# A two-layer model in one kernel: when the expert gather begins, where attention's modulation rows run, and a third raw weight buffer

## The chip, the cores and the metric

The kernel runs on one core of a Trainium2 chip. The metric is the device time of one execution in microseconds (us). Before the change it is 3226.53 us, the median of three runs (3223.47 to 3227.59).

## The reference

Two layers on 512 tokens of width 1024, float32, batch 1. Each layer has a mixer and a PEER feed-forward part, and each of these four parts has a norm whose shift, scale and gate are worked out from a conditioning vector `c` (its 3072 outputs are 24 rows of 128, "modulation rows", in what follows).

```python
def ada_modulation(c, w, b):
    mod = jax.nn.silu(c) @ w + b
    shift, scale, gate = jnp.split(mod, 3, axis=-1)
...
for layer in range(DEPTH):
    shift, scale, gate = ada_modulation(c, mw, mb)      # of the mixer's norm
    h = rms_norm(x, g) * (1.0 + scale) + shift
    x = x + gate * mixer(h, ...)    # layer 0: rglru_mixer, layer 1: fox_mixer
    shift, scale, gate = ada_modulation(c, mw, mb)      # of the feed-forward's norm
    h = rms_norm(x, g) * (1.0 + scale) + shift
    x = x + gate * peer_ffn(h, ...)
```

`rglru_mixer` is a gated linear recurrence behind a short convolution. `fox_mixer` is causal softmax attention with 16 heads of 64 and a forget gate. The feed-forward part picks 16 of 16384 experts for each token and each of 8 heads:

```python
        cand = (v1[..., :, None] + v2[..., None, :]).reshape(TOKEN_CHUNK, PEER_HEADS, PEER_TOPK * PEER_TOPK)
        top_s, top_c = lax.top_k(cand, PEER_TOPK)
        expert = e1 * PEER_KEYS + e2
        g = jax.nn.softmax(top_s, axis=-1)
        u = jnp.take(expert_u, expert, axis=0)
        act = jax.nn.gelu(jnp.einsum('thkd,td->thk', u, xc), approximate=False)
        return jnp.einsum('thk,thkd->td', g * act, jnp.take(expert_v, expert, axis=0))
```

## The kernel before

**Matmuls and weights.** Every product is made of three: weights and activations are split into a high and a low part, and high×high, high×low and low×high are added up (L275 to L277 in the projections, L847 in the experts' second product). All weights come through one object, `Stream` (L123): SyncE (SP) loads a block into a raw buffer `wraw`, ScalarE (ACT) writes its high part `whi`, VectorE (DVE), or GpSimd (POOL) in the queries, the low part `wlo` (L209, L210). There are two raw buffers and, only in the expert loop, a third (`stream.third`); splits run three blocks ahead of their use.

**Stages** (start times from the trace): a norm, the recurrence `lru` (28 us) and its output projection `out_proj` (210); a norm and `peer` of layer 0 (297); a norm and `fox` of layer 1 (1586) with `out_proj` (1906); a norm and `peer` of layer 1 (1960 to the end). Inside `peer` follow one another: `queries` (projection, scores `sps` against the subkeys, top-k on DVE), the first products of 56 of the 128 chunks of 128 experts ("first ups", stored in DRAM for the loop) beside the routing and the dense gates, and the loop over 128 chunks.

**The loop.** For three of the four tiles of 128 tokens all experts are computed, chunk by chunk, six chunks ahead with the first product (`expert_in`). `gated` (L834) multiplies a chunk's activations `at` with its gates, which come back from DRAM in tiles `gtile` of 8 chunks, 1.5 MB, loaded by SP (L818); then ACT and DVE make `wh` (L838) and `wl` (L840). The fourth token tile gathers its experts' rows instead (`gathered`): 128 indirect DMAs of 512 KB for u and 128 for v, issued by POOL (L766) into a ring of eight buffers with the tag "gat", and a pinned DVE instruction for each (L772, L782).

**Background work.** Generators give up work piece by piece: `bg.pump(credit)` draws pieces until their costs (1.2 for a row) have used up the credit. The gather is drawn in the loop, with 3.75 for a chunk that needs its first product and 1.15 for a stored one (`PUMP`). Modulation rows are made by `mod_gen` (L159): a 512 KB load `mw` and a DVE dot product (L174) for each row, with a small operation that puts the result in a column (L178 to L181). Layer 1's mixer norm (`l1_mix`) gets its first 16 rows in layer 0's queries (loaded by SP) and its 8 gate rows in `fox` (loaded by POOL, one buffer), followed there by 18 rows of `l1_ffn`. `row_of` (L187) sends the gate through DRAM: SP writes `line`, POOL loads it back, spread over the partitions, as `grow` (L193).

**Order.** A scheduler reorders instructions on each engine, except for those marked with `keep_in_program_order`, which keep their order among themselves: the dot products, the gather's DVE instructions, the norm's `rs` on POOL (L230) and the first two `gated`.

Of the kernel before, what the change touches and what calls it, by code (L numbers as in the profile page):

```python
# [4 lines left out]
F32 = mybir.dt.float32  # L5
# [29 lines left out]
NEARLY = 16  # L35
PUMP = (3.75, 1.15)
AHEAD = 6
# [85 lines left out]
class Stream:  # L123
# [11 lines left out]
    def fill(self, last):  # L135

        g, nc = self.g, self.g.nc
        last = min(last, len(self.blocks) - 1)
        while len(self.parts) <= last:
            (src, shape, n), b = self.blocks[len(self.parts)]  # L140
            if b == 0:
                self.loads += 1
                src_pool = self.third if self.third and self.loads % 3 == 0 else g.wraw
                self.raw = src_pool.tile([128, n, *shape], F32, name="wraw", tag="wraw")
                nc.sync.dma_start(self.raw, src)
            raw = self.raw[:, b]
            hi = g.wsp.tile([128, *shape], F32R, name="whi", tag="whi")
            lo = g.wsp.tile([128, *shape], F32R, name="wlo", tag="wlo")
            split(g, hi, lo, raw, nc.gpsimd if self.on_pool else nc.vector)
            self.parts.append((hi, lo))  # L150
# [7 lines left out]

def mod_gen(g, pool, mwT, sub, rows, bufs=2, pin=True, queue=None):  # L159

# [4 lines left out]
    def load(r):  # L165
        wf = pool.tile([128, D], F32, name="mw", tag="gat", bufs=bufs)
        (queue or nc.sync).dma_start(wf, mwT[r])
        return wf
# [132 lines left out]

def out_proj(g, psum, y, nk, grow, bg):

    T = g.nc.tensor
    yhi, ylo = y
    load_x(g)
    for half in range(2):
        acc = [psum.tile([128, 512], F32, name=f"oacc{half}{t}") for t in range(TC)]
        pairs = [(k, min(2, nk - k)) for k in range(0, nk, 2)]
# [61 lines left out]
def lru(g, h, conv, bias, lam, during, grow_fn, after):  # L371
# [3 lines left out]
    with pool(tc, name="lruy", bufs=1) as ly:  # L375
        yhi = ly.tile([128, NR, S], F32R, name="yhi")
        ylo = ly.tile([128, NR, S], F32R, name="ylo")
        with pool(tc, name="lru", bufs=1) as lp, pool(tc, name="lruw", bufs=2) as lw:
# [27 lines left out]
            with pool(tc, name="lps", bufs=4, space=PSUM) as psum, \  # L406
                    pool(tc, name="lps2", bufs=2, space=PSUM) as psum2:
                bg = Background(*during(lw))
                ge = {}
# [35 lines left out]
                head = proj_early(g, psum, h, 2)  # L445
                for j in range(NR):
                    ps = head.pop(0) if head else proj_t(g, psum, h)
                    xp = lw.tile([128, S + 3], F32, name="xp", tag="xp")
# [11 lines left out]
                    ps = head.pop(0) if head else proj_t(g, psum, h)  # L460
                    ge[j] = lw.tile([128, S], F32, name="ge", tag="ge", bufs=4)
                    A.activation(ge[j], ps, AF.Gelu)
# [6 lines left out]
        with pool(tc, name="mw", bufs=2) as mw, pool(tc, name="ops", bufs=1, space=PSUM) as psum:  # L469
            out_proj(g, psum, (yhi, ylo), NR, grow, Background(*after(mw)))  # L470


def finish_mixer(g, y, nk, grow, after):

    with pool(g.tc, name="ysp", bufs=1) as yp, pool(g.tc, name="mw", bufs=2) as mw, \
            pool(g.tc, name="ops", bufs=1, space=PSUM) as psum:
        yhi = yp.tile([128, nk, S], F32R, name="yhi")
        ylo = yp.tile([128, nk, S], F32R, name="ylo")
        for k in range(nk):
            split(g, yhi[:, k, :], ylo[:, k, :], y[:, k, :])  # L480
        out_proj(g, psum, (yhi, ylo), nk, grow, Background(*after(mw)))

# [53 lines left out]

def peer(g, h, u, v, grow_fn, during, nd):

# [7 lines left out]
    with pool(tc, name="pk", bufs=1) as pk:  # L546
# [32 lines left out]
        def queries(pw, pa, psum):  # L579

            early, todo = [], []
            bg = Background(*during(pw))

            def scores(hd, w, qh, ql, skh, skl):
# [10 lines left out]
            for hd in range(PH):  # L595
                if hd == 0:
                    early = proj_early(g, psum, h, 2)
                for w in range(2):
                    ps = early.pop(0) if early else proj_t(g, psum, h)
                    if w:  # L600
                        sk = g.stream.take()
                        scores(*todo.pop(), *sk)
                    qh = pw.tile([128, S], F32R, name="qh", tag="qh", bufs=3)
                    ql = pw.tile([128, S], F32R, name="ql", tag="ql", bufs=3)
                    split(g, qh, ql, ps)
                    todo.append((hd, w, qh, ql))
                    if w == 0 and hd > 0:
                        search(hd - 1)
                for c in ups_after(hd):
                    first_up(pa, psum, c)  # L610
                    if todo:
                        scores(*todo.pop(), *sk)
                    bg.pump(1.2)
            bg.finish()
            g.stream.on_pool = False
# [142 lines left out]
        def gathered(t, out):  # L758
# [5 lines left out]
            def fetch(src, j):  # L764
                rows = env["gat"].tile([128, D], F32, name="rows", tag="gat")
                nc.gpsimd.indirect_dma_start(out=rows, out_offset=None, in_=src,  # L766
                                             in_offset=bass.IndirectOffsetOnAxis(ap=ei[:, j:j + 1], axis=0))
                return rows
            for j in range(128):
                r = fetch(u, j)  # L770
# [3 lines left out]
            A.activation(act, act, AF.Gelu)  # L774
            V.tensor_mul(act, act, gt)
            for j in range(128):
                r = fetch(v, j)
# [12 lines left out]
        for t in range(nd, TC):  # L790
            rest.append([])
            late.append(gathered(t, rest[-1]))
        with pool(tc, name="pa", bufs=2) as pa, pool(tc, name="ups", bufs=3, space=PSUM) as psum:
            with pool(tc, name="qw", bufs=2) as qw:
                queries(qw, pa, psum)
            natural(g, psum, h, TC - 1, hn)
            grow = grow_fn()
            with pool(tc, name="pu", bufs=1) as pu, pool(tc, name="pw", bufs=2) as pw:
                todo = []
                bg = Background(*[route(t) for t in range(TC)], *[dense_gates(t, pu, pw, psum, todo) for t in range(nd)])  # L800
                for c in FIRST[NEARLY:]:
                    first_up(pa, psum, c)
                    bg.pump(GP)
                bg.finish()
        rguard.__exit__(None, None, None)
        with pool(tc, name="vw", bufs=2) as vw, pool(tc, name="vps", bufs=2, space=PSUM) as psum:
# [3 lines left out]
            pad(g, vw, 384)  # L810
            g.stream.third = vw
            bg = Background(*late)
# [17 lines left out]
            def gated(c):  # L830
# [7 lines left out]
                pin(A.activation(wh, at, AF.Copy))  # L838
                ready[c] = (wh, wl)
                return lambda: V.tensor_sub(wl, at, wh)  # L840

# [8 lines left out]
            def pump(i):  # L850
                bg.pump(PUMP[1] if stored(i // 2) else PUMP[0])

# [264 lines left out]
def model(tc, *aps):  # L1117
# [4 lines left out]
    with ExitStack() as ctx:  # L1122
# [17 lines left out]

        def mod(p, pool, rows=(*first, *gate), bufs=2, queue=tc.nc.gpsimd):
            return mod_gen(g, pool, a[p + "_mw"], mods[p], rows, bufs, bufs < 8, queue)

# [17 lines left out]
        with pool(tc, name="mw0", bufs=8) as mw:  # L1161
# [3 lines left out]
            lambda p: (mod("l0_mix", p, gate, MB), mod("l0_ffn", p, first[:M0], MB)), grow("l0_mix"), lambda p: (mod("l0_ffn", p, (*first[M0:], *gate)),))  # L1165
        peer(g, normed("l0_ffn"), flat("l0_u"), flat("l0_v"), grow("l0_ffn"), lambda p: (mod("l1_mix", p, first, 2, tc.nc.sync),), 3)
        fox(g, normed("l1_mix"), *arg("fox_", "fb", "qg", "kg"), lambda p: (mod("l1_mix", p, gate, 1), mod("l1_ffn", p, (*first, *gate)[:M2], 1)),
            grow("l1_mix"), lambda p: (mod("l1_ffn", p, (*first, *gate)[M2:]),))
        peer(g, normed("l1_ffn"), flat("l1_u"), flat("l1_v"), grow("l1_ffn"), lambda p: (), 3)
        drop_x(g)  # L1170
# [95 lines left out]
```

## Time and profile before

| what | value |
|---|---|
| median of the runs, us | 3226.53 |
| the profiled execution's own time, us | 3225.38 |
| its span, us | 3223.6 |
| layer 0: queries, first ups and gates, loop (starts, us) | 297, 497, 725 |
| layer 1: queries, first ups and gates, loop (starts, us) | 1960, 2147, 2373 |
| data moved by DMA | 818.97 MB, 254 GB/s on average |
| the gathers' issues of u and of v rows (POOL busy), us | 365.2 and 367.0 |

Times count from the start of the span. A row of the windows view has, behind the stretch and its length, the busy time of PE (TensorE), PEld (its weight loads), DVE, ACT and POOL in it with the count of instructions, then the clock that TensorE was granted (1.00 is full), the mean busy share of the 16 DMA engines (a little over 1 where packets overlap) and the GB/s that they moved. A row of the waits view names who waited for whom, for how long in total, how often, and the longest wait. A row of the timeline has start, length, engine and instruction, and in brackets the idle time ahead of it. `PE vacc L847 <- DVE wl L840` means that the matmul of line 847 into `vacc` waited for the VectorE instruction of line 840 that writes `wl`.

### The profile page before, as it was taken

The numbers are of one execution on the slowest core, as the hardware profiler recorded it, in microseconds if no ns is written. First come the engines' busy times: TensorE is split into PE (matmuls) and PEld (weight loads), VectorE is DVE, ScalarE is ACT, GpSimd is POOL, SyncE is SP. The second block draws the span as 40 slices with busy tenths as digits, with TensorE's granted clock in tenths as the row PEclk, the third lists the DMA queues.
The fourth block names the chain that finished last, engine by engine and source line by source line (L and its number), as shares of the span: only waits on it lengthen the run. The fifth ranks groups of instructions, "written<-read, shape, count | busy, mean of one in ns | idle before, by whom it ended". The sixth has DMA issues, their size and how long they took to land.

```text
span 3223.6 us, 44230 instructions
## 1 busy us (share of the span) xinstructions
PE 3082.9 (96%) x16192; PEld 2702.7 (84%) x16192; DVE 2578.9 (80%) x5230; ACT 1465.8 (45%) x2057; POOL 986.2 (31%) x825
## 2 busy tenths in 40 slices
PE   6998989998999999999999989999989999999999
PEld 5777889988888888888776768899978888888887
DVE  7776899997787888887568976789869788888884
ACT  5773226783333333333357743246853333333332
POOL 1002430005454544441011104430026454444430
PEclk9999999999999999999999989999999999999999
DMA  6454444679999999996332343235799999999983
GB/s 264 136 178 170 165 146 153 240 279 396 365 341 353 348 342 346 347 342 238 116 116 80 113 158 125 100 138 202 270 339 383 366 349 342 348 333 360 334 307 135
DMA packets 304778, 818.97 MB, mean 254 GB/s; under 512 B 27824, under 2 KB 156848, under 8 KB 276016
## 3 DMA queue, kind: packets, MB, share of 16 engines
q1 hardware_dynamic: 175408, 398.22, 35.0%
q0 software_dynamic: 84800, 304.65, 25.1%
q10 hardware_dynamic: 44352, 113.27, 9.3%
q8 instruction: 127, 2.08, 0.2%
q14 instruction: 91, 0.75, 0.1%
HBM read 735.03 MB, written 81.02 MB: 253 GB/s over the span
## 4 chain that ended last, share of the span: by engine, by line
PE 43%; DMA 2%; DVE 2%; issue 2%; ACT 2%; POOL 0%; DVEq 0%; ACTq 0%; POOLq 0%; SPq 0%
PE vacc L847 16%; PE pacc L277 7%; PE pacc L275 7%; PE pacc L276 7%; PE gps L727 1%; DMA gtile<-gscr 1%; DMA gscr<-st 0%; PE oacc L315 0%; PE vacc L953 0%; PE oacc L317 0%; PE oacc L316 0%; PE vacc L955 0%; PE vacc L954 0%; PE tp L1086 0%; ACT st L729 0%
## 5 line engine op out<-in xcount | busy, mean ns | idle before, releaser
L209 ACT ACTIVATE whi<-wraw 128x1024 fp32r<-128x1024 f32 (+2 forms) x646 | 666.1, 1034 | 764.5 <-PE pacc L276 349.8
L275 PE MATMUL pacc<-hhi,whi 128*128 128x384 f32 (+1 forms) x2632 | 931.5, 354 | 17.3 <-ACT at L828 9.0
L277 PE MATMUL pacc<-hhi,wlo 128*128 128x384 f32 (+1 forms) x2632 | 926.5, 352 | 5.2 <-DVE wlo L210 5.1
L276 PE MATMUL pacc<-hlo,whi 128*128 128x384 f32 (+1 forms) x2632 | 924.7, 351 | 0.0
L210 DVE TENSOR_TENSOR wlo<-wraw,whi 128x1024 fp32r<-128x1024 f32 (+1 forms) x566 | 683.2, 1210 | 229.0 <-ACT whi L209 215.7
L847 PE MATMUL vacc<-whi,wh 128*128 128x512 f32 x1536 | 603.5, 393 | 6.6 <-ACT wh L838 6.6
L847 PE MATMUL vacc<-wlo,wh 128*128 128x512 f32 x1536 | 606.3, 395 | 0.0
L847 PE MATMUL vacc<-whi,wl 128*128 128x512 f32 x1536 | 597.3, 389 | 1.5 <-DVE wl L840 1.5
L275 PEld LDWEIGHTS pacc<-hhi,whi 128*128 128x128 f32 x2632 | 500.9, 190 | 46.2 <-ACT at L828 9.3
L277 PEld LDWEIGHTS pacc<-hhi,wlo 128*128 128x128 f32 x2632 | 499.8, 190 | 31.5 <-DVE wlo L210 6.9
L276 PEld LDWEIGHTS pacc<-hlo,whi 128*128 128x128 f32 x2632 | 500.9, 190 | 29.3 <-issue 2.8
L766 POOL DMA_INDIRECT rows<-in_l_v_dram,ei x256 | 367.0, 1434 | 408.2 <-DVE accg L782 361.5
L766 POOL DMA_INDIRECT rows<-in_l_u_dram,ei x256 | 365.2, 1427 | 365.3 <-DVE rows L772 298.1
L838 ACT ACTIVATE wh<-at 128x384 fp32r<-128x384 f32 x256 | 133.9, 525 | 699.4 <-PE vacc L847 346.0
L847 PEld LDWEIGHTS vacc<-whi,wh 128*128 128x128 f32 x1536 | 288.9, 188 | 68.6 <-ACT wh L838 6.9
L847 PEld LDWEIGHTS vacc<-whi,wl 128*128 128x128 f32 x1536 | 289.0, 188 | 67.0 <-DVE wl L840 2.4
L847 PEld LDWEIGHTS vacc<-wlo,wh 128*128 128x128 f32 x1536 | 289.5, 188 | 52.6
L782 DVE SCALAR_TENSOR_TENSOR accg<-rows,act,accg 128x1024 f32<-128x1024 f32 x254 | 324.6, 1278 | 0.5
L772 DVE SCALAR_TENSOR_TENSOR rows<-rows,hn 128x1024 f32<-128x1024 f32 x256 | 304.6, 1217 | 0.0
L834 DVE TENSOR_TENSOR at<-at,gtile 128x384 f32<-128x384 f32 x256 | 140.6, 552 | 144.0 <-DMA at<-ascr 120.9
L210 POOL TENSOR_TENSOR wlo<-wraw,whi 128x1024 fp32r<-128x1024 f32 (+1 forms) x80 | 169.9, 2134 | 212.4 <-ACT whi L209 202.8
L729 ACT ACTIVATE st<-gps 128x512 f32<-128x512 f32 x192 | 185.1, 1109 | 42.0 <-PE gps L727 38.1
(268 smaller groups left out, 3397.2 us busy)
## 6 DMA issues: line engine op xcount, KB each, us to landing
wraw<-in_l_uT_dram SPq DMA_DIRECT2D x128, 1024.0 KB
wraw<-in_l_v_dram SPq DMA_DIRECT2D x128, 1024.0 KB
gscr<-st ACTq DMA_DIRECT2D x48, 1024.0 KB
gtile<-gscr SPq DMA_DIRECT2D x32, 1536.0 KB
mw<-in_l_ffn_mw_dram POOLq DMA_DIRECT2D x48, 512.0 KB
ascr<-at ACTq DMA_DIRECT2D x112, 192.0 KB
at<-ascr ACTq DMA_DIRECT2D x112, 192.0 KB
mw<-in_l_mix_mw_dram SPq DMA_DIRECT2D x32, 512.0 KB
```

Of the source, the lines that this page charges most:

```text
L209: g.nc.scalar.activation(hi, raw, AF.Copy)
L210: (eng or g.nc.vector).tensor_sub(lo, raw, hi)
L275: nc.tensor.matmul(ps, whi[:, k, :], hhi[:, k, :n], start=(k == 0), stop=False)
L276: nc.tensor.matmul(ps, whi[:, k, :], hlo[:, k, :n], start=False, stop=False)
L277: nc.tensor.matmul(ps, wlo[:, k, :], hhi[:, k, :n], start=False, stop=(k == KD - 1))
L729: A.activation(st[:, :, q * 4:q * 4 + 4].rearrange("p e t -> p t e"), gps, AF.Copy, scale=1.0 / GSCALE)
L766: nc.gpsimd.indirect_dma_start(out=rows, out_offset=None, in_=src, in_offset=bass.IndirectOffsetOnAxis(ap=ei[:, j:j + 1], axis=0))
L772: V.scalar_tensor_tensor(r, r, 1.0, hn, op0=OP.mult, op1=OP.mult, accum_out=act[:, j:j + 1]))
L782: tc.keep_in_program_order(V.scalar_tensor_tensor(acc, r, w, acc, op0=OP.mult, op1=OP.add))
L834: pin(V.tensor_tensor(at.rearrange("p (b t) -> p b t", t=16), at.rearrange("p (b t) -> p b t", t=16), gts[c // 8][:, :, c % 8, :], op=OP.m ...
L838: pin(A.activation(wh, at, AF.Copy))
L847: T.matmul(acc[t][d], x[:, ts], y[:, d, :], start=(i == 0 and x is wh and y is vh), stop=(i == PK - 1 and x is wl))
```

## The change

Four things are changed.

1. The gather of a layer waits for the loop's first gated chunk: a POOL copy into `act` reads that chunk's `at`, and it and the first eight u fetches are kept in program order.
2. All 24 rows of `l1_mix` move into layer 0's gather, between its u and its v rows; they use the gather's ring and POOL's queue, four loads ahead. Layer 0's credits are raised to 4.05 and 1.25 (`PUMPS`).
3. Every third load gets a third raw buffer in more stages: the recurrence (with three instead of four `ge` buffers), the first half of the output projections, and the queries and first ups (off for the last six).
4. In the queries the split of `ps` into `qh` and `ql` is written ahead of the scores of the half before.

```diff
-PUMP = (3.75, 1.15)
+PUMPS = ((4.05, 1.25), (3.75, 1.15))
...
-                src_pool = self.third if self.third and self.loads % 3 == 0 else g.wraw
-                self.raw = src_pool.tile([128, n, *shape], F32, name="wraw", tag="wraw")
+                raw, bufs = g.wraw, 2
+                if self.third and self.loads % 3 == 0:
+                    raw, bufs = self.third
+                self.raw = raw.tile([128, n, *shape], F32, name="wraw", tag="wraw", bufs=bufs)
...
-def mod_gen(g, pool, mwT, sub, rows, bufs=2, pin=True, queue=None):
+def mod_gen(g, pool, mwT, sub, rows, bufs=2, pin=True, queue=None, ring=None):
...
-        wf = pool.tile([128, D], F32, name="mw", tag="gat", bufs=bufs)
+        wf = pool.tile([128, D], F32, name="mw", tag="gat", bufs=ring or bufs)
...
+        g.stream.third = None if half else (third, 1)
...
+                g.stream.third = (lw, 1)
...
-                    ge[j] = lw.tile([128, S], F32, name="ge", tag="ge", bufs=4)
+                    ge[j] = lw.tile([128, S], F32, name="ge", tag="ge", bufs=3)
...
+                    qh = pw.tile([128, S], F32R, name="qh", tag="qh", bufs=3)
+                    ql = pw.tile([128, S], F32R, name="ql", tag="ql", bufs=3)
+                    split(g, qh, ql, ps)
                     if w:
                         sk = g.stream.take()
                         scores(*todo.pop(), *sk)
-                    qh = pw.tile([128, S], F32R, name="qh", tag="qh", bufs=3)
-                    ql = pw.tile([128, S], F32R, name="ql", tag="ql", bufs=3)
-                    split(g, qh, ql, ps)
...
-                    bg.pump(1.2)
-            bg.finish()
...
-                nc.gpsimd.indirect_dma_start(out=rows, out_offset=None, in_=src,
-                                             in_offset=bass.IndirectOffsetOnAxis(ap=ei[:, j:j + 1], axis=0))
+                i = nc.gpsimd.indirect_dma_start(out=rows, out_offset=None, in_=src,
+                                                 in_offset=bass.IndirectOffsetOnAxis(ap=ei[:, j:j + 1], axis=0))
+                if src is u and j < 8:
+                    tc.keep_in_program_order(i)
                 return rows
+            tc.keep_in_program_order(nc.gpsimd.tensor_copy(act[:, 127:128], env["first"][:, 0:1]))
...
+            if between:
+                yield from between(env["gat"])
...
+            g.stream.third = (pa, 1)
...
+                    if c == FIRST[-6]:
+                        g.stream.third = None
...
-            g.stream.third = vw
+            g.stream.third = (vw, 2)
...
+                env.setdefault("first", at)
...
-                bg.pump(PUMP[1] if stored(i // 2) else PUMP[0])
+                bg.pump(cost[1] if stored(i // 2) else cost[0])
...
-        peer(g, normed("l0_ffn"), flat("l0_u"), flat("l0_v"), grow("l0_ffn"), lambda p: (mod("l1_mix", p, first, 2, tc.nc.sync),), 3)
-        fox(g, normed("l1_mix"), *arg("fox_", "fb", "qg", "kg"), lambda p: (mod("l1_mix", p, gate, 1), mod("l1_ffn", p, (*first, *gate)[:M2], 1)),
+        peer(g, normed("l0_ffn"), flat("l0_u"), flat("l0_v"), grow("l0_ffn"), lambda p: mod("l1_mix", p, bufs=4, ring=8), 3, PUMPS[0])
+        fox(g, normed("l1_mix"), *arg("fox_", "fb", "qg", "kg"), lambda p: (mod("l1_ffn", p, (*first, *gate)[:M2], 1),),
             grow("l1_mix"), lambda p: (mod("l1_ffn", p, (*first, *gate)[M2:]),))
-        peer(g, normed("l1_ffn"), flat("l1_u"), flat("l1_v"), grow("l1_ffn"), lambda p: (), 3)
+        peer(g, normed("l1_ffn"), flat("l1_u"), flat("l1_v"), grow("l1_ffn"), None, 3, PUMPS[1])
```

DVE in layer 0's queries, one of the places where modulation rows (`mw`, `mdot`, `col_l_mix`) stand within the search for the best candidates (`cand`), before:

```order
L561 MAX_INDEX idxs_2427<-vals_2425,tk 128x8
L174 SCALAR_TENSOR_TENSOR mw,mdot<-mw,sc 128x1024
L572 TENSOR_TENSOR cand<-vals_2425,vals_2424 128x4x16
L181 TENSOR_TENSOR col_l_mix_147<-mdot,bias_l_mix 128x1
L174 SCALAR_TENSOR_TENSOR mw,mdot<-mw,sc 128x1024
L572 TENSOR_TENSOR cand<-vals_2425,vals_2424 128x4x2 x2
L178 TENSOR_SCALAR mdot<-mdot,bias_l_mix 128x1
L572 TENSOR_TENSOR cand<-vals_2425,vals_2424 128x4x2
L574 TENSOR_TENSOR cand<-vals_2424,vals_2425 128x4x8
```

The same place in the changed kernel:

```order
L567 MAX_INDEX idxs_2427<-vals_2425,tk 128x8
L578 TENSOR_TENSOR cand<-vals_2425,vals_2424 128x4x16
L578 TENSOR_TENSOR cand<-vals_2425,vals_2424 128x4x2 x3
L580 TENSOR_TENSOR cand<-vals_2424,vals_2425 128x4x8
L563 MAX top<-cand 128x8 x2
```

The dot products and their column operations are gone from between the candidates; the rest stands as it was. The order of `qh` and `ql` (L210, now L212) among these instructions hasn't moved.

DVE at the start of layer 0's loop, before (`at_7477` is chunk 0's tile, `rows` a gathered row, `act` its results):

```order
L210 TENSOR_TENSOR wlo<-wraw,whi 128x1024 x4
L834 TENSOR_TENSOR at_7541<-at_7541,gtile 128x384
L772 SCALAR_TENSOR_TENSOR rows,act<-rows,hn 128x1024 x2
L210 TENSOR_TENSOR wlo<-wraw,whi 128x1024
L772 SCALAR_TENSOR_TENSOR rows,act<-rows,hn 128x1024
L210 TENSOR_TENSOR wlo<-wraw,whi 128x1024
L834 TENSOR_TENSOR at_7477<-at_7477,gtile 128x384
```

And in the changed kernel, where `at_7389` is chunk 0's tile:

```order
L212 TENSOR_TENSOR wlo<-wraw,whi 128x1024 x4
L844 TENSOR_TENSOR at_7453<-at_7453,gtile 128x384
L212 TENSOR_TENSOR wlo<-wraw,whi 128x1024 x2
L844 TENSOR_TENSOR at_7389<-at_7389,gtile 128x384
L844 TENSOR_TENSOR at_7486<-at_7486,gtile 128x384
L212 TENSOR_TENSOR wlo<-wraw,whi 128x1024
L851 TENSOR_TENSOR wl<-at_7389,wh 128x384
L844 TENSOR_TENSOR at_7420<-at_7420,gtile 128x384
L777 SCALAR_TENSOR_TENSOR rows,act<-rows,hn 128x1024 x2
```

The first gathered rows now stand behind four gated chunks instead of one.

POOL in the second half of `fox`, before, where `qx` and `kx` are loads that the attention's heads need:

```order
L167 DMA mw<-in_l_mix_mw_dram 128x1024 x2
L167 DMA mw<-in_l_ffn_mw_dram 128x1024
L1046 DMA qx<-cx 4x512 x2
L193 DMA grow<-line 128x1024
L1057 DMA kx<-cx 4x512 x2
```

POOL in layer 0's loop and at the norm behind it, in the changed kernel:

```order
L773 COPY act<-at_7389 128x1
L768 DMA rows<-in_l_u_dram,ei 128x1024 x128
L169 DMA mw<-in_l_mix_mw_dram 128x1024 x24
L768 DMA rows<-in_l_v_dram,ei 128x1024 x128
L195 DMA grow<-line 128x1024
L232 TENSOR_TENSOR rs<-ms,mhalf 128x1 x4
```

The copy stands ahead of all gathers, the 24 `mw` loads between u and v, and `grow` has moved out of `fox` to just ahead of the norm's four `rs`.

More of the change, by code (lines that the diff above doesn't have):

```diff
@@ L299, in out_plan, with out_proj @@
     return plan
-def out_proj(g, psum, y, nk, grow, bg):
+def out_proj(g, psum, y, nk, grow, bg, third):
     T = g.nc.tensor
@@ L446, in lru @@
                 for j in range(NR):
+                    if j == NR - 1:
+                        g.stream.third = None
                     ps = head.pop(0) if head else proj_t(g, psum, h)
@@ L469, in lru @@
         with pool(tc, name="mw", bufs=2) as mw, pool(tc, name="ops", bufs=1, space=PSUM) as psum:
-            out_proj(g, psum, (yhi, ylo), NR, grow, Background(*after(mw)))
+            out_proj(g, psum, (yhi, ylo), NR, grow, Background(*after(mw)), mw)
 def finish_mixer(g, y, nk, grow, after):
@@ L480, in finish_mixer @@
             split(g, yhi[:, k, :], ylo[:, k, :], y[:, k, :])
-        out_proj(g, psum, (yhi, ylo), nk, grow, Background(*after(mw)))
+        out_proj(g, psum, (yhi, ylo), nk, grow, Background(*after(mw)), mw)
 def atanh2(g, out, u, u2):
@@ L534, in peer_plan, with peer @@
     return plan
-def peer(g, h, u, v, grow_fn, during, nd):
+def peer(g, h, u, v, grow_fn, between, nd, cost):
     tc, nc = g.tc, g.nc
@@ L581, in queries @@
             early, todo = [], []
-            bg = Background(*during(pw))
             def scores(hd, w, qh, ql, skh, skl):
@@ L801, in peer @@
                 for c in FIRST[NEARLY:]:
+                    if c == FIRST[-6]:
+                        g.stream.third = None
                     first_up(pa, psum, c)
@@ L1139, in model, with mod @@
         gate = range(16, 24)
-        def mod(p, pool, rows=(*first, *gate), bufs=2, queue=tc.nc.gpsimd):
-            return mod_gen(g, pool, a[p + "_mw"], mods[p], rows, bufs, bufs < 8, queue)
+        def mod(p, pool, rows=(*first, *gate), bufs=2, queue=tc.nc.gpsimd, ring=None):
+            return mod_gen(g, pool, a[p + "_mw"], mods[p], rows, bufs, bufs < 8, queue, ring)
         def grow(p):
```

## The prediction

> **What bounds the kernel now.** I read the page's first two parts, then cut the span into stages with the windows view, and asked the waits view, stage by stage, which wait of TensorE ends last.
>
> ```profile
> span 3223.6 us, 44230 instructions
> PE 3082.9 (96%) x16192; PEld 2702.7 (84%) x16192; DVE 2578.9 (80%) x5230; ACT 1465.8 (45%) x2057; POOL 986.2 (31%) x825
> PEclk9999999999999999999999989999999999999999
> DMA  6454444679999999996332343235799999999983
> ```
>
> TensorE is busy for 3082.9 of 3223.6 us and the order of its matmuls in the PEER stages is the same before and after. So no edit here can shorten the work itself; an edit gains only where TensorE idles or runs at a lowered clock, and those places are few. Everything below is a list of such places. The sum is made against the profiled execution's own time, 3225.38 us (span 3223.6 and 1.8 around it); the median of the runs shown, 3226.53, lies 1.1 above it.
>
> **Term 1, layer 0's queries: 16 modulation rows go.** Both layers run the same matmuls here, and layer 1 has no modulation rows in this stage, so the trace holds its own control:
>
> ```profile
> 297.00:497.00 200.00, 188.65 (x977) 171.62 (x976) 173.17 (x891) 59.87 (x82) 87.67 (x89) 0.94 0.39 139
> 1960.00:2147.00 187.00, 181.76 (x976) 165.22 (x976) 140.76 (x841) 59.32 (x81) 86.99 (x90) 0.98 0.30 111
> PE sps L590 <- DVE ql L210: 11.1, 3, 4.7
> PE sps L590 <- DVE ql L210: 4.4, 1, 4.4
> L174 DVE SCALAR_TENSOR_TENSOR mw<-mw,sc 128x1024 f32<-128x1024 f32 x14 | 16.9, 1210 | 0.0
> ```
>
> The columns are length, busy time of PE, its loads, DVE, ACT and POOL, the granted clock, DMA share and GB/s. The same 976 matmuls take about 199.5 us in layer 0 (297.2 to 496.7) and 187.4 in layer 1. DVE has 32 us more to do, 19.4 of it the sixteen dot products of 1.21 us (14 of them inside this window), and the query splits `ql` queue behind them: three waits of TensorE (11.1 us) against one (4.4), and a mean clock of 0.94 against 0.98. With the rows gone, DVE's order in layer 0 is that of layer 1, where the last of the three waits stands as well. I take **−12**; bounds −16 (all three waits, with the clock behind them) and −6 (two waits alone). The moved split lines in the source are worth 0: the two `ql` stand in DVE's order where they stood.
>
> **Term 2, the start of the two expert loops.**
>
> ```profile
> 725.00:763.00 38.00, 28.24 (x147) 27.72 (x148) 15.04 (x21) 11.36 (x16) 15.60 (x13) 0.87 1.03 392
> 732.34 0.38 SPq L818 DMA_DIRECT2D gtile<-gscr  x1
> 730.86 1.04 POOL L766 DMA_INDIRECT rows<-in_l_u_dram,ei  x1 [9.89 <-PE pacc L277]
> 740.14 0.94 POOL L766 DMA_INDIRECT rows<-in_l_u_dram,ei  x1 [0.30 <-issue]
> DVE at L834 <- DMA gtile<-gscr: 14.4, 1, 14.4
> PE pacc L275 <- ACT at L828: 9.0, 1, 9.0
> 2381.11 21.06 DMA gtile<-gscr
> PE vacc L847 <- ACT wh L838: 6.6, 1, 6.6
> 741.00:746.00 5.00, 5.00 (x31) 5.00 (x30) 0.00 (x0) 0.00 (x0) 0.09 (x1) 1.00 1.04 410
> 756.00:761.00 5.00, 5.00 (x16) 5.00 (x17) 5.00 (x8) 1.63 (x3) 3.22 (x3) 0.50 1.06 389
> 2408.50:2416.50 8.00, 6.54 (x15) 4.67 (x16) 8.00 (x14) 2.59 (x5) 5.60 (x4) 0.50 1.02 418
> ```
>
> SP issues the gate tile at 732.34, while POOL issues the first eight gathers of 512 KB each (730.86 to 740.14, 4.2 MB). The DMA engines are full (share 1.03), and in layer 1 the 1.5 MB gate tile takes 21.06 us from issue to landing, 75 GB/s of the 392 that move. DVE waits 14.4 us for it and TensorE 9.0 and 6.6. Behind each gap the clock is 0.50: 16 matmuls in 5 us where 31 ran, 2.5 us lost in layer 0, and half of the 6.5 busy us in layer 1, 3.3. Held back, the gather takes 4.2 MB out of the gate tile's way, 4.2/0.392 = 10.7 us, and the tile lands at about 744 and not 755, ahead of the 746.8 at which TensorE runs dry. So the gap goes: 9.0 + 2.5 = 11.5 us in layer 0, 6.6 + 3.3 = 9.9 in layer 1.
>
> But the bytes don't go, and these rows say how much is kept:
>
> ```profile
> 755.00:775.00 20.00, 19.17 (x85) 17.56 (x86) 20.00 (x32) 8.34 (x14) 12.98 (x9) 0.85 1.05 404
> 795.00:815.00 20.00, 20.00 (x96) 17.32 (x95) 15.78 (x26) 4.50 (x6) 14.73 (x10) 1.00 1.05 407
> ACT whi L209 <- DMA wraw<-in_l_v_dram: 10.5, 1, 10.5
> PE pacc L277 <- DVE wlo L210: 2.3, 1, 2.3
> 2485.00:2525.00 40.00, 40.00 (x198) 35.59 (x197) 34.73 (x53) 14.50 (x20) 19.39 (x14) 1.00 0.99 374
> ```
>
> From 755 to 815 the engines stay full, DVE is full until about 795, and a weight load then arrives so late that ACT waits 10.5 us (800 to 837) and TensorE 2.3 at 833. A TensorE that comes 11.5 us earlier meets that load sooner. In layer 1 they are full until 2525. I keep 40 to 50%: **−5 in each layer**, since the share falls to 0.89 at 815 and some of the shortage is paid off there. Bounds for each: all kept (−11.5 and −9.9) and +3 (all given back, and the start of the third raw buffer or the rows' catch-up a little worse).
>
> The Trainium skill, "DMA: Bandwidth & Descriptors", section "Issuing engines are not separate DMA queues", says that transfers issued by different engines share 16 DMA engines and interleave; the trace agrees (two streams together at 1.03). By that alone a held-back gather only trades places with the weights and this term would be 0, which is my first rival.
>
> **Term 3, layer 0's loop takes up 24 modulation rows.**
>
> ```profile
> 763.00:1572.00 809.00, 805.79 (x3887) 709.62 (x3886) 647.22 (x833) 284.14 (x390) 352.12 (x244) 1.00 0.89 329
> L772 DVE SCALAR_TENSOR_TENSOR rows<-rows,hn 128x1024 f32<-128x1024 f32 x256 | 304.6, 1217 | 0.0
> 800.00:1400.00 600.00, 288.89 (x202) 1.00 0.94 348
> ```
>
> 24 dot products of the gather's own form, 1.22 us each with some 0.1 for the column, are 31 us more of DVE in 809 (80% becomes 84%), under a TensorE that is busy for 805.8. 24 × 512 KB are 12.6 MB more: 329 GB/s becomes 345 over the stage, and 348 becomes 364 in the middle, where the share is already 0.94. The start shows 392 to 407, so it fits. The credits rise with the work: I count 351 given over the loop's 124 steps against 336 needed, last reached at step 117 (before: 325 against 307, step 116), so the gather doesn't run over the loop's end. I take **+4**, near to the row of 407; bounds 0 (all hidden) and 12.6/0.348 = +36 (no byte more than now).
>
> **Term 4, attention loses 8 rows and the gate's trip through DRAM.**
>
> ```profile
> 1586.00:1906.00 320.00, 302.89 (x1404) 228.52 (x1403) 251.52 (x573) 203.97 (x404) 36.62 (x69) 0.96 0.31 106
> L174 DVE SCALAR_TENSOR_TENSOR mw<-mw,sc 128x1024 f32<-128x1024 f32 x26 | 31.7, 1218 | 10.1 <-DMA mw<-in_l_ffn_mw_dram 5.0 <-DMA mw<-in_l_mix_mw_dram 4.8
> 1738.46 9.29 DMA line<-gate_l_mix
> 1749.84 5.17 DMA mw<-in_l_ffn_mw_dram
> PE tp L1086 <- DVE col_l_ffn L179: 4.1, 1, 4.1
> 1757.70:1767.70 10.00, 10.00 (x30) 6.91 (x29) 6.30 (x16) 5.61 (x14) 1.03 (x2) 0.50 0.17 54
> 1860.00:1906.00 46.00, 35.15 (x155) 26.33 (x153) 35.92 (x102) 20.07 (x54) 3.79 (x7) 0.81 0.40 144
> 1860.00:1906.00 46.00, 6.81 (x12) 3.79 (x7) 0.81 0.40 144
> ```
>
> The chain that ended last runs through one place here: the last l1_mix row ends, `line` is written (9.29 us), POOL stands at `grow<-line`, and the next `mw` load is queued behind it on POOL (5.17 us). DVE, pinned, holds the softmax behind that row, and TensorE waits 4.1 us and then runs 10 us at half clock: 9.1 us, which go whole, since `grow` now follows the gather. The remaining 18 of 26 rows end by softmax chunk 42 of 64 where they ran to the last two. In the tail (1860 to 1906) TensorE idles for 46 − 35.2 = 10.9 us and has a mean clock of 0.81, while DVE spends 6.8 us on `mw` tiles (the last row, which counts those alone); I take 6, a little less than DVE gets back. Together **−15**; bounds −25 and 0 (TensorE's order changes here too, and a new knot may take the old one's place).
>
> **Term 5, the rest.**
>
> ```profile
> 1572.00:1586.00 14.00, 6.67 (x33) 5.96 (x34) 9.98 (x27) 6.35 (x11) 2.94 (x4) 0.79 0.42 150
> 28.00:210.00 182.00, 169.64 (x715) 135.21 (x716) 148.53 (x270) 135.07 (x175) 11.34 (x21) 0.97 0.52 171
> ```
>
> The norm ahead of attention now has POOL issue `grow` ahead of its four `rs`; the issue alone is about 0.5 us and comes while the last experts run, unless its transfer is waited for: +1, bounds 0 and +6 (the `mw` transfer's 5.17). The recurrence, where TensorE idles for 12.4 us in 182, gets the third raw buffer and three more activation table loads, and one `ge` buffer less: −1, bounds −7 and +6. The third buffer in the output projections and the first ups is in these bounds too.
>
> Sum: −12 − 5 − 5 + 4 − 15 + 1 − 1 = −33, and 3225.4 − 33 = **3192**.
>
> **The rivals.**
> - *The loop starts give all back.* The DMA engines are full for 80 us, the bytes are conserved, and a load at 817 is already late. Against: the share falls to 0.89 right behind. Term 2 is 0: 3202. Chance 0.2.
> - *All of term 2 is kept* (the catch-up of 100% on DVE at 755 to 795 came only from the wait, and vanishes with it): 21 us and not 10, 3181. Chance 0.15.
> - *Attention is re-knotted.* Its order on TensorE changes, and another pinned row or the `p`, `tp` ping-pong takes the 4 us gap's place: term 4 is 0, 3207. Chance 0.12.
> - *Layer 0's loop turns DMA-bound* (the other side). If no more than 348 GB/s can be had from gathers and weights mixed, the 12.6 MB cost 36 us, and waits of over 2 us each bring a lowered clock, some 25 us more over ten of them: 3192 − 4 + 61 = 3249. It decides from the point where the share would pass 1.0, that is, if under 12.6 MB/809 us = 16 GB/s are left. Against: 392 to 407 in the start. Chance 0.05.
> - *The change doesn't do what it says*: for the moved `ql` lines this is so, and priced at 0. The copy that should hold the gather reads chunk 0's gated tile, and POOL's order puts the gathers behind it, so the hold itself is real.
>
> **How the numbers follow.** Forecast 3192 with 0.48 (3183 to 3199), the rivals as given. Below, all of term 2 (11 more) with terms 1 and 4 at their ends (4 and 10 more) and half of the recurrence's gain (4 more) give 3163; above, the loop starts and attention failing together (10 and 15) give 3217. The range is 3163 to 3217; it leaves out the fourth rival and the corners. About 0.2% (6.5 us) is what a measurement of this kernel can tell from no change; faster by more than that needs a time under 3220: 0.92. Within: 0.04; slower: 0.04, most of the fourth rival.
>
> **What would show it.** Term 1: layer 0's queries last 187 to 188 us, one `ql` wait. Term 2: no `gtile` wait of over 3 us on DVE at either start, the clock at 1.0, and in exchange `wlo` waits in the 90 us behind. Term 3: DMA 345 GB/s over layer 0's loop, TensorE still over 99% busy. Term 4: no gap of 4 us in mid-attention, no `mw` in the last third of the softmax. I'd be wrong if layer 0's loop shows many `wlo` or `wl` waits, if the gate tile still takes 20 us (the weights then fill the engines without the gather), or if attention keeps its 320 us.

## The result

The changed kernel takes 3169.33 us (median of four runs, 3163.85 to 3176.52) against 3225.0 before (median of four runs); the ratio is 0.9829 with a 95% interval of 0.9806 to 0.9851. The forecast was 3192, the range 3163 to 3217. So the sign and the order of size were right, and the gain is 56 us where 33 were forecast. The time lies inside the range, near its lower end, but below the 3183 to 3199 that were thought likeliest and below every rival. On another chip the same kernel gave 0.9848 (0.983 to 0.9865).

From the page of the changed kernel, the rows that were shown first of the kernel before:

```profile
span 3169.2 us, 44257 instructions
PE 3067.4 (97%) x16192; PEld 2692.0 (85%) x16192; DVE 2586.4 (82%) x5230; ACT 1465.9 (46%) x2060; POOL 990.2 (31%) x843
PEclk9998999999999999999999999999999999999999
DMA  7444334779999999997332234245699999999983
```

TensorE's count of matmuls is unchanged and its busy time fell by 15.5 us, since fewer of them run at half clock (the mean granted clock is 0.985 against 0.979). The table gives the length of each stage, from the first matmul of one to that of the next, in the profile of each kernel (e1 to e4 are experiments described below; "again" is a second profile of the changed kernel).

| stage, us | before | changed | again | e1 hold alone | e2 no hold | e3 rows alone | e4 third alone |
|---|---|---|---|---|---|---|---|
| recurrence | 182.3 | 180.5 | 179.9 | 182.5 | 180.3 | 183.3 | 179.7 |
| its output projection | 77.0 | 81.1 | 78.0 | 74.1 | 79.6 | 76.7 | 76.8 |
| layer 0: queries | 199.5 | 186.7 | 185.6 | 198.8 | 186.3 | 186.6 | 196.6 |
| layer 0: first ups, gates | 227.8 | 225.2 | 224.4 | 228.8 | 225.4 | 225.5 | 227.2 |
| layer 0: loop with its start | 852.8 | 845.0 | 843.2 | 842.4 | 853.5 | 848.1 | 849.3 |
| attention | 320.5 | 301.7 | 299.0 | 320.2 | 299.2 | 300.4 | 319.8 |
| layer 1: queries | 187.4 | 187.4 | 185.9 | 187.3 | 185.4 | 186.6 | 187.3 |
| layer 1: loop with its start | 850.9 | 836.6 | 844.2 | 848.2 | 847.8 | 847.7 | 850.3 |

The two profiles of one kernel show how far a single stage may be trusted: within 2 us in layer 0's loop, but 8 us apart in layer 1's, 3 us in the projection and in attention. So a loop's few us are read from several kernels or from the medians. The profile of e1 is of the slowest of its four runs (3211.45).

**Layer 0's queries.** The windows and the waits of the changed kernel (the window view's columns as before):

```profile
299.00:485.00 186.00, 181.88 (x973) 165.40 (x973) 150.88 (x837) 59.08 (x80) 86.36 (x89) 0.98 0.33 113
PE sps L594 <- DVE ql L212: 4.1, 1, 4.1
```

It now is layer 1's stage: one `ql` wait, clock 0.98.

**The loops' starts.** From the timelines of SP and POOL, the waits between 700 and 740 and between 740 and 870, and the windows:

```profile
717.96 0.38 SPq L828 DMA_DIRECT2D gtile<-gscr  x1
733.00 0.36 POOL L773 COPY act<-at 128x1 f32<-128x1 f32 x1 [26.64 <-DVE at L844]
733.85 1.06 POOL L768 DMA_INDIRECT rows<-in_l_u_dram,ei  x1 [0.48 <-issue]
DVE at L844 <- DMA gtile<-gscr: 3.7, 1, 3.7
PE pacc L279 <- DVE wlo L212: 4.0, 3, 1.9
740.00:760.00 20.00, 19.54 (x98) 17.17 (x97) 18.03 (x27) 5.29 (x7) 15.82 (x12) 1.00 1.02 418
760.00:780.00 20.00, 20.00 (x99) 17.69 (x98) 20.00 (x34) 7.08 (x10) 16.59 (x11) 1.00 1.02 419
```

The gate tile is issued at 717.96 and the first gather now at 733.85, behind it. DVE waits 3.7 us for the tile and not 14.4 (a little over the 3 that I had set as a sign), TensorE no longer waits for `at`, and the clock in these windows is 1.00. Behind it the engines carry 418 GB/s, more than the 404 before, and what TensorE waits for weights is 4.0 us in three pieces.

**The loop and attention.**

```profile
737.00:1556.00 819.00, 807.19 (x3892) 710.14 (x3891) 689.07 (x942) 285.80 (x394) 375.96 (x281) 1.00 0.93 348
1564.00:1866.00 302.00, 294.12 (x1406) 224.72 (x1404) 243.15 (x550) 202.98 (x406) 31.35 (x60) 0.98 0.29 98
1820.00:1866.00 46.00, 42.49 (x218) 33.56 (x215) 37.03 (x94) 30.45 (x72) 1.10 (x2) 0.96 0.35 123
PE s L1085 <- ACT p L1092: 4.0, 3, 3.4
1775.80:1782.60 6.80, 6.73 (x20) 4.38 (x21) 4.07 (x15) 5.14 (x14) 0.55 (x1) 0.50 0.22 78
```

The 24 rows raised the loop's rate from 329 to 348 GB/s and DVE's busy time by 42 us in a window 10 us longer, and TensorE stayed busy: of the 11.8 us that it idles in this window, 7.1 are the wait for the norm at the loop's end. In attention DVE has 8 us less to do, but the stage is 19 us shorter: the wait behind `grow` is gone, and in the last 46 us TensorE is busy for 42.5 us at 0.96 where it was for 35.2 at 0.81. One stop is left in mid-attention, at another place: TensorE waits 3.4 us for `p` (the last wait shown), and then runs at a clock of 0.50 for 6.8 us (the last row).

### The profile page after: what moved, and what is told of

Same layout as the page of the kernel before. It is cut to its first block, busy times and chain, and to the rows that moved or that the text cites. A ratio compares the mean times of both kernels' runs of the same rounds, so it can differ in the third digit from the quotient of the medians.

```text
span 3169.2 us, 44257 instructions
## 1 busy us (share of the span) xinstructions
PE 3067.4 (97%) x16192; PEld 2692.0 (85%) x16192; DVE 2586.4 (82%) x5230; ACT 1465.9 (46%) x2060; POOL 990.2 (31%) x843
## 4 chain that ended last, share of the span: by engine, by line
PE 78%; DVE 10%; DMA 5%; ACT 4%; issue 3%; POOL 0%; SPq 0%; DVEq 0%; ACTq 0%; POOLq 0%
PE vacc L858 29%; PE pacc L277 13%; PE pacc L279 13%; PE pacc L278 13%; DVE wlo L212 2%; PE gps L729 2%; DVE rows L777 2%; DMA wraw<-in_l_v_dram 1%; PE oacc L319 1%; ACT st L731 1%; PE oacc L320 1%; PE oacc L318 1%; DMA wraw<-in_lru_out_dram 1%; DVE mw L176 1%; DMA gscr<-st 1%
## 5 line engine op out<-in xcount | busy, mean ns | idle before, releaser
L212 DVE TENSOR_TENSOR wlo<-wraw,whi 128x1024 fp32r<-128x1024 f32 (+1 forms) x566 | 682.4, 1209 | 187.6 <-ACT whi L211 187.2
L777 DVE SCALAR_TENSOR_TENSOR rows<-rows,hn 128x1024 f32<-128x1024 f32 x256 | 304.4, 1217 | 11.5 <-DMA rows<-in_l_u_dram,ei 11.5
L212 POOL TENSOR_TENSOR wlo<-wraw,whi 128x1024 fp32r<-128x1024 f32 (+1 forms) x80 | 169.6, 2126 | 200.4 <-ACT whi L211 200.3
```

The costliest lines, as they stand in the source:

```text
L212: (eng or g.nc.vector).tensor_sub(lo, raw, hi)
L777: V.scalar_tensor_tensor(r, r, 1.0, hn, op0=OP.mult, op1=OP.mult, accum_out=act[:, j:j + 1]))
```

## The experiments

Twelve kernels were run. The first four take the change apart.

**e1, the hold alone.** The kernel before with the pinned copy and the pinned first fetches:

```diff
+                if src is u and j < 8:
+                    tc.keep_in_program_order(i)
                 return rows
+            tc.keep_in_program_order(nc.gpsimd.tensor_copy(act[:, 127:128], env["first"][:, 0:1]))
...
+                env.setdefault("first", at)
```

> The kernel before with the held gather alone. Theory A (the gain at the loop starts is kept, because the transfers behind still find room): both starts lose their waits, layer 0's start and loop together -11 to -12 us, layer 1's -13 to -14, about 3200 us in all. Theory B (the start is bound by the DMA engines, bytes are conserved, and the changed kernel was fast there because of something else in it): the gaps at the start go but weight waits in the 100 us behind take back half or more, about 3213 us or above.

Measured: 3202.28 against 3220.34 of before, ratio 0.9941 (0.9925 to 0.9958), 18 us. The first two waits are from 700 to 790, the third from layer 1, 2400 to 2520:

```profile
DVE at L837 <- DMA gtile<-gscr: 3.9, 1, 3.9
PE pacc L275 <- ACT st L729: 0.8, 1, 0.8
PE pacc L275 <- ACT whi L209: 6.6, 1, 6.6
```

The 9 us wait for `at` is no longer there. Layer 0 keeps 10.4 us, nearly what theory A says; in layer 1's profile the start is 7 us shorter and the loop behind it 4.5 longer, with one late weight of 6.6 us, as theory B says. The total lies between the theories, nearer to A.

**e2, the changed kernel without the hold** (the lines above taken out of it).

> The changed kernel with the gather free again to start as early as it can. Theory A: the waits for the gate tile of about 14 us (DVE) come back in both layers and the time rises by 22 to 27 us, to 3192-3196. Theory B: it rises by 10 or less, to 3180 or below.

Measured: 3185.38, ratio 0.9893 (0.9876 to 0.9909): by the medians 16 us over the changed kernel, which wasn't measured beside it; by the ratios to the kernel before, 14 us over its second comparison and 21 over its first. The waits are back, the first two in layer 0 and the third in layer 1 (2310 to 2400):

```profile
DVE at L841 <- DMA gtile<-gscr: 12.2, 1, 12.2
PE pacc L277 <- ACT at L835: 9.3, 1, 9.3
PE vacc L854 <- ACT wh L845: 6.2, 1, 6.2
```

Taken by the medians, the hold is worth 18 us alone and 16 within the change: less than the 25 of A, more than the 10 of B.

**e3, the moved rows alone**, with `PUMPS` and the generator `between` in the gather, no hold and no third buffer:

```diff
-            bg = Background(*during(pw))
...
-                    bg.pump(1.2)
-            bg.finish()
...
+            if between:
+                yield from between(env["gat"])
...
```

> The kernel before with the moved modulation rows and layer 0's credits alone. Theory: layer 0's queries -12 to -13 us, attention -19, layer 0's loop +4: 3225 - 28 = 3197. Rival (24 rows overload the loop's transfers unless the start is relieved too): layer 0's loop +15 or more, about 3210. Second rival (a part of attention's 19 us belongs to the third buffer's shift of the weight loads, not to the rows): attention -15 or less.

Measured: 3186.28, ratio 0.9899 (0.9883 to 0.9916), 34 us. Queries −12.9 and attention −20.1 as expected; layer 0's loop, for which +4 was expected, is 4.7 us shorter in this profile. The five profiles whose gather starts early in layer 0 spread over 848 to 854 us there, so this is no gain, but the rival's +15 isn't there either, and neither is the second rival. The first ups lose 2.3 us, which I had not priced: in the kernel before, two of the sixteen rows ran in that stage (497 to 724):

```profile
L174 DVE SCALAR_TENSOR_TENSOR mw<-mw,sc 128x1024 f32<-128x1024 f32 x2 | 2.4, 1210 | 0.0
```

**e4, the third buffer alone.**

```diff
+        g.stream.third = None if half else (third, 1)
...
+                g.stream.third = (lw, 1)
...
+            g.stream.third = (pa, 1)
...
```

> The kernel before with the third raw buffer alone (and three ge buffers). Theory: recurrence -2 us, its output projection +4, first ups -2 to -3, all else as before: within 2 us of 3225. Rival (the buffer is what makes the loop starts cheap, as the weights for the loop are loaded earlier): 10 us or more off the starts, 3212.

Measured: 3215.53 against 3220.34, ratio 0.9982 (0.9971 to 0.9993): 5 us, more than the theory's 2, less than the rival's 10 or more, and the starts are as slow as before (38.3 and 36.1 us for the stretch up to the first `vacc`, 38.0 and 35.8 before). In its profile the recurrence is 2.6 us shorter and layer 0's queries 2.9, but layer 1's queries, with the same buffer, aren't; where the 5 us lie stays open. The three parts add up: 18 + 34 + 5 = 57, against the 48 to 56 us of the changed kernel in its two comparisons.

**e6, the eight gate rows back in attention.**

```diff
-        peer(g, normed("l0_ffn"), flat("l0_u"), flat("l0_v"), grow("l0_ffn"), lambda p: mod("l1_mix", p, bufs=4, ring=8), 3, PUMPS[0])
+        peer(g, normed("l0_ffn"), flat("l0_u"), flat("l0_v"), grow("l0_ffn"), lambda p: mod("l1_mix", p, first, bufs=4, ring=8), 3, PUMPS[0])
-        fox(g, normed("l1_mix"), *arg("fox_", "fb", "qg", "kg"), lambda p: (mod("l1_ffn", p, (*first, *gate)[:M2], 1),),
+        fox(g, normed("l1_mix"), *arg("fox_", "fb", "qg", "kg"), lambda p: (mod("l1_mix", p, gate, 1), mod("l1_ffn", p, (*first, *gate)[:M2], 1)),
```

> The changed kernel with the eight gate rows of l1_mix back in attention (one buffer, POOL's queue), the sixteen others still in layer 0's gather. Theory: the chain from the last of these rows over line, grow and the next mw load comes back, with its wait and half clock (9 us), and DVE's extra rows cost the rest: attention goes from 302 back to 316-321 us, the whole to about 3186. Rival (the gain in attention came from the later start or another order of the matmuls, not from the gate rows): attention stays under 308 us.

Measured: 3188.32, ratio 0.9904 (0.9887 to 0.992). Attention takes 321.8 us, so the whole of its gain is the gate rows'. Its windows (all of attention, its last 46 us) and waits:

```profile
1559.00:1882.00 323.00, 304.26 (x1409) 229.03 (x1408) 252.69 (x575) 205.36 (x407) 36.49 (x69) 0.95 0.31 108
1836.00:1882.00 46.00, 35.43 (x155) 26.57 (x154) 36.01 (x103) 20.46 (x54) 3.78 (x7) 0.81 0.45 167
PE tp L1097 <- DVE col_l_ffn L181: 5.3, 1, 5.3
PE tp L1097 <- DVE p L1094: 4.8, 3, 2.1
```

The stand in mid-attention and the slow tail are both back, with the tail's busy time, matmul count and clock as before.

**e11, the same with `grow` held back behind the last row's load.**

```diff
+        if bufs == 1:
+            g.tc.keep_in_program_order(i)
...
-    nc.gpsimd.dma_start(row, bcast_rows(line, 128, D))
+    g.tc.keep_in_program_order(nc.gpsimd.dma_start(row, bcast_rows(line, 128, D)))
```

> The kernel with the eight gate rows in attention (attention 322 us, 3188 in all) again, but with these mw loads and grow in program order on POOL, so that grow comes behind the last mw load and holds none of them up. Theory (my term: the stand behind grow and its half clock are 9 us, the rest is DVE's work): attention 311 to 314, the whole about 3178. Rival A (the stand is the whole of it): 300 to 304. Rival B (the rows' own time on DVE and their one buffer are all of it): 319 or more.

Measured: 3182.89, ratio 0.9888 (0.9873 to 0.9903); attention 315.8 us.

```profile
1825.00:1871.00 46.00, 36.70 (x168) 28.91 (x167) 37.31 (x99) 23.08 (x56) 4.08 (x8) 0.81 0.55 197
PE tp L1099 <- DVE p L1096: 7.9, 5, 2.6
L178 DVE SCALAR_TENSOR_TENSOR mw<-mw,sc 128x1024 f32<-128x1024 f32 x5 | 6.1, 1222 | 0.1
DVE mw L178 <- DMA mw<-in_l_ffn_mw_dram: 4.3, 1, 4.3
PE o L1105 <- DVE ptl L214: 3.7, 2, 3.5
```

The wait on `col_l_ffn` has gone, and attention is 6 us shorter. But a stop stays at nearly the same place though `grow` now comes last: DVE waits 4.3 us for a row's load (5.7 in e6), and TensorE 3.5 us for `ptl` behind it. So e11 doesn't take the whole stand out, and why that load is late isn't shown. The tail is nearly as slow as in e6, with five rows' dot products in it; in the changed kernel none stands in those 46 us.

The traces split attention's loss without this run. The table adds up TensorE's idle time and half of the time for which it was busy at a clock of 0.50:

| lost in attention, us | before | e6 | e11 | changed | again |
|---|---|---|---|---|---|
| ahead of the last 46 us | 12.1 | 13.1 | 10.3 | 7.8 | 6.8 |
| in the last 46 us | 17.5 | 17.2 | 15.1 | 5.1 | 3.5 |

So 4 to 5 us were gained in mid-attention and 12 to 14 in the tail.

**e7, twice the rows in layer 0's loop**: each of the 24 is loaded and worked out twice, with credits to match (4.4 and 1.35).

```diff
-                yield from between(env["gat"])
+                for _ in range(2):
+                    yield from between(env["gat"])
```

> The changed kernel with each of the 24 modulation rows loaded and worked out twice in layer 0's loop (credits 4.4 and 1.35), so 12.6 MB and 31 us of DVE more. Theory (DMA engines and DVE have room): layer 0's start and loop together 845 becomes 847 to 853 us. Rival (the loop is at the edge of what the DMA engines carry): 865 us or more, the whole at 3190 or above.

Measured: 3182.64, ratio 0.9881 (0.9862 to 0.99), 13 us over the changed kernel beside it. Layer 0's loop with its start takes 860.0 us, 15 to 17 more, between theory and rival. Two windows, of each first "again", then e7, and e7's longest wait in the first:

```profile
800.00:1000.00 200.00, 197.61 (x949) 174.07 (x948) 178.15 (x275) 70.61 (x98) 111.69 (x78) 0.99 1.00 385
800.00:1000.00 200.00, 191.37 (x905) 168.23 (x904) 180.10 (x279) 69.69 (x97) 124.35 (x82) 0.97 1.01 385
PE vacc L859 <- DVE wl L852: 4.9, 1, 4.9
1000.00:1200.00 200.00, 200.00 (x974) 177.05 (x973) 171.60 (x259) 70.52 (x97) 76.10 (x72) 1.00 0.97 358
1000.00:1200.00 200.00, 200.00 (x967) 176.08 (x966) 178.31 (x314) 68.38 (x96) 65.52 (x77) 1.00 0.99 373
```

The time isn't lost where the rows are. POOL issues all 48 loads between 1021 and 1143 us, and from 1000 to 1200 the engines carry 373 GB/s against 358 while TensorE is busy for all 200 us. It is lost ahead of them, from 800 to 900 us, and once more near 1200, where POOL issues gathers alone, drawn faster by the higher credits: from 800 to 1000 it issued 82 of them against 78, and the same 385 GB/s was carried. So in this profile the added rows had room, and the denser gather didn't. No run had one without the other, and a denser gather is the price of more rows in this loop.

**e9, the hold in layer 1 alone.**

```diff
+                if src is u and j < 8 and not between:
...
+            if not between:
+                tc.keep_in_program_order(nc.gpsimd.tensor_copy(act[:, 127:128], env["first"][:, 0:1]))
```

> The changed kernel with the gather held in layer 1 alone; in layer 0 it starts as early as it can. Together with the kernels without any hold (+16) and with both this splits the hold's worth. If both layers keep three quarters: +7 to +9 us over the changed kernel. If layer 0, with its denser credits, gives its part back: within 3 us of the changed kernel. If layer 1 gives its part back: +14 or more.

Measured: 3176.63 (3168.15 to 3183.14), ratio 0.9861 (0.9839 to 0.9883), 7 us over the changed kernel beside it. In layer 0 DVE waits 12.9 us for the tile and TensorE 9.9 again:

```profile
DVE at L845 <- DMA gtile<-gscr: 12.9, 1, 12.9
PE pacc L277 <- ACT at L839: 9.9, 1, 9.9
```

The four runs spread over 15 us, and the interval meets that of the changed kernel beside it (0.983 to 0.9865), so the medians alone don't split the hold. The stages do it better: over the profiles, layer 0's loop with its start takes 848.1 to 854.1 us in the five kernels without the hold there (mean 852) and 839.9 to 845.0 in the eight with it, e7 left out (mean 843); layer 1's takes 847.7 to 850.9 in four without (mean 849) and 836.6 to 848.2 in ten with it (mean 841). That is some 9 us of 11.5 in layer 0 and 8 of 9.9 in layer 1, so each layer keeps about four fifths; the kernels differ in their other parts too, and layer 1's profiles overlap.

**e5, no third buffer in the output projections**, and **e8**, the changed kernel once more.

```diff
-        g.stream.third = None if half else (third, 1)
```

> The changed kernel without the third raw buffer in the output projections. Layer 0's output projection took 78 to 81 us in the kernels with all parts of the change against 77 before. Theory (the buffer there starts loads that come at a bad time): it returns to 77, the whole is 1 to 4 us shorter than the changed kernel's 3169. Rival (the spread of that stage is chance): within 1 us, the stage still at 78 to 81.

> The changed kernel itself, to measure on one chip with the others and to see how far its stages differ from one profile to the next. Theory: within 6 us of 3169, with differences of 2 to 4 us in each loop.

Measured: e5 3167.76, ratio 0.9844 (0.9831 to 0.9857); e8 3169.44, ratio 0.9848 (0.983 to 0.9865). The whole can't be told from e8. But e5's projection took 74.8 us, and the profiles side with the theory there: layer 0's projection takes 74.1 to 77.0 us in the four kernels without the buffer (mean 75.7) and 76.7 to 81.1 in the ten with it (mean 78.7). The buffer seems to cost 3 us at this place.

**e10 and e12, fewer rows due at the start.**

```diff
-                bg.pump(cost[1] if stored(i // 2) else cost[0])
+                bg.pump((cost[1] if stored(i // 2) else cost[0]) * (0.75 if i < 16 else 1.0))
```

> The changed kernel with three quarters of the credits in the first 16 chunks of both loops, so that fewer gathered rows are due while the DMA engines are full; the gather still ends by chunk 122 of 124. Theory (what is left of the wait for weights in the first 150 us of the loops comes from this crowding): layer 0's start and loop 844 becomes 839 to 841 us, layer 1's 837 to 844 becomes 836 to 840, the whole 3162 to 3166. Rival (rows put off are missed at the end, or the weights alone fill the engines there): within 2 us of 3169 or above.

e12 has 0.5 in place of 0.75, and `PUMPS = ((4.3, 1.3), (3.95, 1.2))`.

> The changed kernel with half of the credits in the first 16 chunks of both loops, and higher credits (4.3 and 1.3, 3.95 and 1.2) so that the gather still ends by chunk 121. Theory (the crowding at the start is not yet gone with three quarters of the credits): 3156 to 3160, no weight wait of over 1 us in the first 150 us of a loop. Rival (three quarters was enough, and the rows put off only crowd the rest of the loop): 3161 or above.

Measured: e10 3161.48 (3158.89 to 3162.79), ratio 0.982 (0.9807 to 0.9834), each of its five runs shorter than each of e5's five on the same chip (3164.26 to 3171.36), which differs from the changed kernel by the projections' buffer. e12 3163.08, ratio 0.9814 (0.9801 to 0.9827), so no further gain that could be told; its theory's 3156 to 3160 didn't come. Windows from 755 to 815 of "again", e10 and e12:

```profile
755.00:815.00 60.00, 57.61 (x272) 50.58 (x271) 56.38 (x90) 20.45 (x29) 41.82 (x29) 0.97 1.04 414
755.00:815.00 60.00, 58.41 (x283) 51.15 (x282) 53.73 (x83) 21.19 (x31) 37.88 (x24) 1.00 0.99 385
755.00:815.00 60.00, 60.00 (x292) 52.88 (x291) 51.64 (x79) 23.53 (x34) 30.02 (x20) 1.00 0.97 370
```

Fewer gathered rows, less traffic, and a TensorE that is busier: the crowding at the start is real. From 735 to 885 TensorE waits 3.2 us in "again", 2.3 in e10 and not at all in e12. These two have the lowest medians of the study, by the ratios 3 to 11 us below the changed kernel, but the stages don't place e10's gain there: its loops take 843.4 us in layer 0 (839 to 841 were expected) and 837.5 in layer 1, within the changed kernel's two profiles. What made e10 faster stays open. In e12 they take 839.9 and 838.0.

## Why the prediction came out as it did

- **Term 1 (−12): right.** Measured −12.8 and −13.9 in two profiles, −12.9 with the rows alone, and one `ql` wait stays. The control inside the same trace gave the size. That same control also had the first ups at 227.8 against 225.6, which I didn't compare; it was another 2.3 us.
- **Term 2 (−5 in each layer): the mechanism right, the size half.** The gap and its half clock went as worked out (11.5 us in layer 0). What failed is the step "I keep 40 to 50%": e1 and e2 show 16 to 18 us kept of the 21.4 I had worked out, and the stage lengths 17. I had argued that the DMA engines are full from 755 to 815 and that bytes are conserved. Two things were missing in this. A share at or over 1 isn't one rate: 404 GB/s before became 418 once the gather came later. That is the smaller part: 14 GB/s over 40 us are 0.6 MB, an estimate of 1.4 us. And the weights had been arriving early: in the trace of before the low parts of the weights stood ready 8.9 us (median, 775 to 825) ahead of the first matmul that reads them, in the changed kernel 4.6 (755 to 805). With the hold alone it is 4.6 (e1, 765 to 815), without it in the changed kernel 8.8 (e2). So the lead goes with the hold, by about 4 us; that the advance was paid from it is my reading. That not all of the loss was avoided shows in the 4.0 us of `wlo` waits in layer 0, and in the 6.6 us of e1's layer 1.
- **Term 3 (+4): right within what can be told.** Layer 0's loop is 1 to 3 us longer with everything than with the hold alone. The bound of +36 was far off for these rows, and in e7 as many bytes again were carried without a wait of TensorE where they stood; what cost 15 us there were the denser gathers around them.
- **Term 4 (−15): two sizes off, in opposite ways.** The stand in mid-attention was taken at 9.1, "which go whole". It went, but another stop of 3.4 us came up at `p`, so 4 to 5 us were gained there; and e11 shows that `grow` was only a part of the stand. The tail was taken at 6, "a little less than DVE gets back", and is 12 to 14. The step that failed most is to price the tail by DVE's 6.8 us: with the late rows TensorE loses 17.5 us there, 11.1 in gaps and 6.4 at half clock (0.81 against 0.96 in the last 46 us), and without them 3.5 to 5.1. I had the row with the 0.81 and counted DVE's time only.
- **Term 5 (0): a little too high.** The third buffer alone is worth 5 us (2 to 9 by its interval), where I had taken 1. `grow` ahead of `rs` costs about what I had taken: the wait ahead of the norm's first transpose is 7.1 us where it was 5.5, in all kernels that have `grow` there.
- **The rivals.** Of those with a chance, the one that kept all of term 2 came nearest. A DMA-bound loop is excluded by its length (845.0 against 852.8 before), the starts giving all back by e1 and e2. Attention was re-knotted in part: the stop at `p` is new, but it costs 5 to 7 us (3.4 and half of the 3.4 or 6.8 at half clock), not the 15 of the rival. The chain of the sum is 33 + 7 (term 2) + 5 (term 4) + 2 (first ups) + 4 (third buffer) = 51, against 56 in the first comparison and 48 in the second.

## What to carry to other kernels

Where a small transfer that the next stage waits for is issued beside a large one that is only prefetch, hold the large one until the small one has been used: here that was worth 16 to 18 us in two loops for one copy and a few pinned instructions. Before you count such a gain as given back because the DMA engines are full, look at how far ahead of use the next loads arrive: that lead can pay. And price background work at the end of a stage by what the waiting TensorE loses in gaps and clock, not by the background's own time.

## What the runs showed of the hardware that I had not expected

The busy share of the DMA engines doesn't tell the rate: at a share of 0.97 to 1.04 the windows shown here have 358 to 419 GB/s, with 414 at 1.04 and 419 at 1.02. And a gap costs TensorE twice, at a price that changes from run to run: behind the 3.4 us stop in the changed kernel's attention the clock was 0.50 for 6.8 us, and behind the same stop in "again" for 3.4.
